# A two-layer encoder: one wide split in place of four, and the first pair of quads finished behind the second pair's second product

## The chip, the cores and the metric

The kernel runs on one core of a Trainium2 chip. The metric is device microseconds of one execution; lower is better. The core has five engines with queues of their own, each of which runs its instructions strictly in the order in which they were written for it: PE (matrix products), DVE and POOL (elementwise work), ACT (elementwise work with a table of functions, and copies out of PE's accumulators), and SP, which here only starts transfers. Between engines the order is kept by semaphores: an instruction whose operand isn't there holds everything behind it on its engine.

## The reference, cut to what matters

1024 tokens of width 1024 go through two layers. Each layer is a mixer (a Fourier group, windowed attention and attention to a memory, normed by groups and multiplied with `w_out`) and a gated feed-forward part, each between two RMS norms and with a residual:

```
for l in range(2):
    h = rmsnorm(x, g_pre_mix);  ...  x = x + rmsnorm(y @ w_out, g_post_mix)
    h = rmsnorm(x, g_pre_ffn[l])
    gate, up = split(h @ w_ffn_in[l])          # 1024 -> 2 * 2816
    x = x + rmsnorm((silu(gate) * up) @ w_ffn_out[l], g_post_ffn[l])
```

All is float32. The kernel multiplies float32 as three products of a faster type: each operand is split into `hi` (a cast on ACT) and `lo` (operand minus `hi`, on DVE), and PE adds hi·hi, hi·lo and lo·hi.

## The kernel before, in words

The feed-forward products go by a scheme of seven half-size products in place of eight (Strassen's). The normed activations, turned so that the 1024 features lie on partitions, are seven moving blocks `hb.b[1..7]` of 512 features by 512 tokens, each as hi and lo. Blocks 1, 2 and 3 are plain quarters, 5, 6, 7 and 4 are differences. Class `Blocks` (lines 1079 to 1123) makes them. `tile` turns one tile of 128 tokens; the first four tiles (half 0) are stored raw (`raw[0]`, `raw[1]`), the last four give blocks 5, 3 and 6 piece by piece. `plain` splits one 128-token piece of a raw quarter for block 1 or 2. `rest` makes blocks 7 and 4, four pieces each: a subtraction on DVE (line 1122), then cast and subtraction for hi and lo (lines 176 and 177).

A `Quad` (lines 1127 to 1217) is 256 columns of `w_ffn_in`. It does seven products in the order `ORDER = (1, 2, 5, 6, 3, 7, 4)`, each of 12 matmuls of 128x512. Ahead of a product `weights` makes its stationary operand: for 5, 6, 3 and 7 a running sum on DVE (line 1159), then again cast and `lo`, into a ring of slots `wcs` (four of them while the first two pairs run). A slot is only rewritten once the product that read it is done. `snap` copies an intermediate product out of the accumulator (ACT, line 1176) into a ring `sns`, and `step` combines them: lines 1208, 1211 and 1216 on DVE, 1205 and 1212 on POOL.

Two quads, gate and up, are a pair; there are 11 pairs a layer. `gate_out` (line 1223) takes silu of the gate quad's four results, `up_out` (lines 1227 to 1247) multiplies them with the up quad's, forms the seven blocks for the second product and sends them to memory `actd`.

The first two pairs overlap the end of the mixer. Per token tile the mixer's last product (`mo`, 24 matmuls) is followed by two norms: L1070, a square on ACT (L360), two small operations on POOL, L362, L363, a square on ACT (L314), POOL again, L319, and then PE turns the tile (`hTp`, line 1104). The products 1 and 2 of the first pair (`qc`) and of the second (`qa`) stand among the last tiles; then come 5 (`qy`), 6 (`qx`), 3 (into `qy`), 7 (into `qx`) and 4 (`qz`) of the first pair and of the second. The weights of the first pair are loaded by `load_part` (line 1136), where the destination has to come free first: a part of them into rows that the residual uses, the second pair's into the place of a weight of `mo`.

The order on each engine isn't the order of the source. A scheduler places each instruction by a model of the engines; `tc.issue_after(x)` keeps what is in it behind instruction x in the order. So an edit in one place can move instructions elsewhere, and what each queue holds is read from the built program, below.

## Time and profile before

| | |
|---|---|
| median of 3 runs | 2057.03 us (2054.72 to 2058.41) |
| profiled execution | 2054.33 us, of which the span of instructions is 2052.6 us |
| PE busy | 1994.2 us of the span (97%) |
| DVE, ACT, POOL busy | 1506.6, 1051.2, 699.9 us |
| mean granted clock of PE | 0.989 |
| layer 0: end of the mixer and first two pairs | about 385 to 480 us |
| layer 1: the same stage | about 1390 to 1480 us |

The profile is one execution. Times in it count from the first instruction. A row of the timeline has the start, the duration, the engine, the source line, the operation, and in brackets how long the engine sat idle before it and for what. A row of the stretches ("windows") has, for each engine, the busy time and the number of instructions, then the clock granted to PE (1.00 is full) and the DMA share.

### The profile page before, as it was taken

To read this page: it belongs to the slowest core of one execution; us is meant where nothing else is said; L and a number is where in the kernel's file an instruction comes from. 1 tells how busy PE (TensorE), PEld (TensorE's weight loads), DVE (VectorE), ACT (ScalarE), POOL (GpSimd) and SP (SyncE) were. 2 spreads that over 40 slices of the span, in tenths; PEclk is the share of its full clock that TensorE was granted. 3 is DMA by queue.
4 is the path that set the end of the run, shared out by engine and by line. 5 is a ranking of instruction groups with operands and counts; after the bars stand their busy time and mean duration, and the time that the engine had idled before them with its cause. 6 is when DMAs were issued, how large, how long until landed. Compare 5 with 4: busy or idle time off the path is not lost.

```text
span 2052.6 us, 28381 instructions
## 1 busy us (share of the span) xinstructions
PE 1994.2 (97%) x9587; PEld 1632.0 (80%) x9587; DVE 1506.6 (73%) x2400; ACT 1051.2 (51%) x2238; POOL 699.9 (34%) x819
## 2 busy tenths in 40 slices
PE   8999999999999999999999999999999999999998
PEld 7877777778888888887788768777788888887886
DVE  5557767897767766778866668578886777778766
ACT  6466767643333333554555667685333333345541
POOL 4354445234334333002423544451443433410011
PEclk9999999999999999999999999999999999999999
DMA  6110232433322323979831112243343233269973
GB/s 215 57 57 31 98 103 104 154 113 113 124 98 95 116 83 121 314 267 324 289 127 49 47 62 99 93 146 117 108 139 105 94 110 108 78 208 343 318 271 127
DMA packets 181890, 288.57 MB, mean 141 GB/s; under 512 B 15560, under 2 KB 81648, under 8 KB 181744
## 3 DMA queue, kind: packets, MB, share of 16 engines
q1 hardware_dynamic: 173680, 267.88, 39.0%
q10 hardware_dynamic: 8064, 18.88, 2.4%
q8 instruction: 75, 1.23, 0.2%
q14 instruction: 71, 0.58, 0.1%
HBM read 220.11 MB, written 66.58 MB: 140 GB/s over the span
## 4 chain that ended last, share of the span: by engine, by line
PE 81%; DVE 7%; DMA 4%; issue 3%; ACT 3%; POOL 2%; SPq 0%; DVEq 0%; POOLq 0%; ACTq 0%
PE fo L1319 15%; PE qy L1171 11%; PE qx L1171 11%; PE qc L1171 10%; PE mo L187 7%; PE qz L1171 6%; PE kvp L187 4%; PE qp L187 4%; PE zT L187 2%; DVE arena_r L177 2%; PE sc L785 2%; PE pT L822 2%; DMA arena_f<-actd 1%; PE av L830 1%; PE qa L1171 1%
## 5 line engine op out<-in xcount | busy, mean ns | idle before, releaser
L176 ACT CAST arena_r<-arena_f 128x512 fp32r<-128x512 f32 (+1 forms) x436 | 242.1, 582 | 323.7 <-DVE arena_f L1159 67.4
L1319 PE MATMUL fo<-arena_r 128*128 128x512 f32 x1512 | 353.8, 390 | 5.2 <-ACT big L1344 2.8
L177 DVE TENSOR_TENSOR arena_r<-arena_f,arena_r 128x512 fp32r<-128x512 f32 x354 | 254.5, 745 | 111.1 <-ACT arena_r L176 99.3
L1319 PEld LDWEIGHTS fo<-arena_r 128*128 128x128 f32 x1512 | 283.5, 188 | 64.9 <-ACT big L1344 3.2
L176 ACT CAST flex<-arena_f 128x512 fp32r<-128x512 f32 x210 | 128.7, 621 | 269.6 <-PE qy L1171 67.1
L1171 PE MATMUL qc<-arena_r,flex 128*128 128x512 f32 x912 | 221.0, 390 | 0.0
L1171 PEld LDWEIGHTS qc<-arena_r,flex 128*128 128x128 f32 x912 | 171.1, 188 | 36.8
L177 DVE TENSOR_TENSOR flex<-arena_f,flex 128x512 fp32r<-128x512 f32 x210 | 159.8, 767 | 51.9 <-ACT flex L176 51.1
L1205 POOL TENSOR_TENSOR arena_f<-arena_f 128x512 f32<-128x512 f32 x40 | 54.3, 1359 | 269.5 <-ACT arena_f L1176 269.5
L1171 PE MATMUL qy<-arena_r,flex 128*128 128x512 f32 x576 | 138.4, 390 | 0.0
L1171 PEld LDWEIGHTS qy<-arena_r,flex 128*128 128x128 f32 x576 | 108.0, 188 | 22.9 <-DVE flex L177 0.4
L1171 PE MATMUL qy<-arena_r 128*128 128x512 f32 x480 | 119.2, 397 | 5.4 <-DVE arena_r L177 5.4
L1171 PE MATMUL qx<-arena_r 128*128 128x512 f32 x360 | 119.3, 389 | 0.0
L1171 PEld LDWEIGHTS qy<-arena_r 128*128 128x128 f32 x480 | 91.7, 191 | 25.5 <-DVE arena_r L177 6.3
L1212 POOL TENSOR_TENSOR arena_f<-arena_f 128x512 f32<-128x512 f32 x40 | 66.8, 1670 | 129.6 <-DVE arena_f L1211 125.4
L1171 PE MATMUL qz<-arena_r,flex 128*128 128x512 f32 x320 | 107.4, 398 | 0.0
L1159 DVE TENSOR_TENSOR arena_f<-arena_f 128x512 f32<-128x512 f32 x90 | 97.5, 1084 | 8.5 <-DMA arena_f<-in_w_ffn_in 6.6
L177 POOL TENSOR_TENSOR arena_r<-arena_f,arena_r 128x256 fp32r<-128x256 f32 (+2 forms) x82 | 67.0, 823 | 99.9 <-ACT arena_r L176 74.5
L187 PE MATMUL mo<-big,arena_r 128*128 128x512 f32 x384 | 98.8, 398 | 1.4 <-DVE flex L859 1.3
L1171 PE MATMUL qx<-flex,flex 128*128 128x512 f32 x304 | 100.0, 390 | 0.0
L235 POOL TENSOR_SCALAR rrsv<-rss 128x1 f32<-128x1 f32 x32 | 10.7, 334 | 259.9 <-ACT arena_f L348 197.8
L1300 DVE TENSOR_TENSOR arena_f<-arena_f 128x512 f32<-128x512 f32 x110 | 80.1, 733 | 22.2 <-DMA arena_f<-in_w_ffn_out 21.1
(305 smaller groups left out, 4484.0 us busy)
## 6 DMA issues: line engine op xcount, KB each, us to landing
arena_f<-in_w_ffn_out SPq DMA_DIRECT2D x264, 256.0 KB, 4.6
actd<-arena_f SPq DMA_DIRECT2D x154, 256.0 KB, 2.5
arena_f<-actd SPq DMA_DIRECT2D x154, 256.0 KB, 4.3
arena_f<-in_w_ffn_in SPq DMA_DIRECT2D x46, 512.0 KB, 3.9
big<-in_w_ffn_in SPq DMA_DIRECT2D x40, 512.0 KB, 4.5
arena_f<-in_w_in SPq DMA_DIRECT2D x40, 256.0 KB, 2.9
arena_f<-in_x SPq DMA_DIRECT2D x16, 512.0 KB, 4.3
arena_f<-in_w_out SPq DMA_DIRECT2D x32, 256.0 KB, 2.7
```

What stands on the lines that cost most here:

```text
L176: nc.scalar.copy(hi, src)
L177: return (lo_eng or nc.vector).tensor_tensor(out=lo, in0=src, in1=f32(hi), op=ALU.subtract)
L187: mm(self.dst, a, b, start=self.i == 0, stop=self.i == self.n - 1)
L785: mm(pt, lhs, self.kst[g][i][:, k0 * P : k1 * P], start=i == 0, stop=i == 1)
L822: nc.tensor.transpose(pT[:, h, :], es_[h // 2][:, h % 2, j * P : j * P + P], ident)
L830: mm(av[64 * s : 64 * s + 64, 0 : 2 * P], self.v32[:, k0 + j], rhs, start=j == 0, stop=j == nk - 1)
L1159: nc.vector.tensor_tensor(out=s, in0=x, in1=y, op=op)
L1171: mm(pt, a, b, start=start and n == 0, stop=n == 11, skip_group_check=not start)
L1205: G(out=self.u2, in0=self.u2, in1=self.p1, op=ALU.add)
L1212: G(out=self.p5, in0=self.p1, in1=self.p5, op=ALU.add)
L1300: nc.vector.tensor_tensor(out=s, in0=x, in1=y, op=op)
L1319: mm(pt, ab[:, 0, x, sl], ab[:, 1, y], start=new and first and j == 0, stop=last and j == 2, skip_group_check=not new)
```

## The change

Four things are changed; what is computed stays the same.

1. `rest` makes a whole block with one subtraction of 128x2048 and one wide split, where four pieces of 128x512 had a subtraction and a split each. Block 2 is split whole in the same way (`whole`), behind the last of its tiles; block 1 still goes by pieces.
2. Silu and the products of the first pair are written between products 6 and 3 of the second pair's gate quad, and held behind the cast of the weights of product 6, where they stood behind the first pair. The copies' ring `sns` has eight places in place of six from the second pair on, so that the first pair's copies live on meanwhile.
3. For the first pair, the two additions of `step` that ran on POOL run on DVE.
4. The first running sum of the first pair (product 5) is held behind the last norm that has been written.

```diff
+    normed = [None]
     def norm_x(x, g, h=None, keep=None):
...
-        nc.vector.scalar_tensor_tensor(out=h, in0=x, scalar=r[:, 0:1], in1=g, op0=ALU.mult, op1=ALU.mult)
+        normed[0] = nc.vector.scalar_tensor_tensor(out=h, in0=x, scalar=r[:, 0:1], in1=g, op0=ALU.mult, op1=ALU.mult)
...
+        def whole(self, i, s):
+            self.b[i] = [big(4, 512) if k is None else at(k, 4, 512, dt=F32R) for k in self.HB[i]]
+            split(*self.b[i], s)
+
         def rest(self, kg):
-            for c in range(4):
-                d = self.raw[kg][:, :, c * P : c * P + P]
-                with tc.issue_after(self.lo.ins):
-                    nc.vector.tensor_tensor(out=d, in0=self.s[c], in1=d, op=ALU.subtract)
-                self.put((7, 4)[kg], c, d)
+            d = self.raw[kg]
+            cut = lambda ap: ap.rearrange("p k (c q) -> p k c q", q=P)
+            s = at(8, 4, 4, P).rearrange("p c k q -> p k c q")
+            with tc.issue_after(self.lo.ins):
+                nc.vector.tensor_tensor(out=cut(d), in0=s, in1=cut(d), op=ALU.subtract)
+            self.whole((7, 4)[kg], d)
...
-                nc.vector.tensor_tensor(out=s, in0=x, in1=y, op=op)
+                with tc.issue_after(normed[0].ins) if i == 5 and self.first else ExitStack():
+                    nc.vector.tensor_tensor(out=s, in0=x, in1=y, op=op)
...
-            split(w[:, 0], w[:, 1], s)
+            self.cast = nc.scalar.copy(w[:, 0], s)
+            nc.vector.tensor_tensor(out=w[:, 1], in0=s, in1=f32(w[:, 0]), op=ALU.subtract)
...
-            V, G = nc.vector.tensor_tensor, nc.gpsimd.tensor_tensor
+            V, G = nc.vector.tensor_tensor, (nc.vector if self.first else nc.gpsimd).tensor_tensor
...
             if p == 0:
-                gq, uq = first
-                g = gate_out(gq)
-                up_out(uq, g, actd, p)
-                wsums.ks, sns.ks = (4, 6, 0, 2), (36, 38, 40, 42, 32, 34)
+                wsums.ks, sns.ks, sns.i = (4, 6, 0, 2), (32, 34, 44, 46, 36, 38, 40, 42), 0
                 continue
...
                 for i in ORDER[2:] if p == 1 else ORDER:
+                    if i == 3 and p == 1 and q is gq:
+                        with tc.issue_after(q.cast.ins):
+                            g = gate_out(first[0])
+                        up_out(first[1], g, actd, 0)
                     q.step(i)
...
-                for c in range(4):
-                    hb.plain(1, c)
+                hb.whole(2, hb.raw[1])
```

Line numbers below are each program's own: the changed one's are higher, by 2 in the mixer (L364 is the old L362), by 8 to 11 in the quads (L1130 the wide subtraction, L1168 the running sum, L1171 and L1172 cast and lo of weights, L1181 the matmuls, L1215, L1218, L1221, L1222 and L1226 the old L1205, L1208, L1211, L1212 and L1216). In the rows, `flex_2276` holds the half-difference from which `rest` subtracts, `big_3523` and `big_3530` are the raw quarters, `big_4391` or `big_4376` is the lo of block 4, and `arena_r<-arena_f` or `flex_4102<-arena_f` at 128x512 is the lo of a weight.

The first place is DVE in layer 0 where `rest` runs. Before, from the weights of the first pair's product 4 to the weight of the second pair's product 5 (the last row):

```order
L177 TENSOR_TENSOR flex_4102<-arena_f,flex_4102 128x512
L177 TENSOR_TENSOR big_4391<-big_3530,arena_r 128x4x128
L1122 TENSOR_TENSOR big_3530<-flex_2276,big_3530 128x4x128
L1232 TENSOR_TENSOR arena_f<-qc_4147,flex_2276 128x512
L1208 TENSOR_TENSOR arena_f<-qy_4292,arena_f 128x512
L177 TENSOR_TENSOR flex_4102<-arena_f,flex_4102 128x512
L177 TENSOR_TENSOR big_4391<-big_3530,arena_r 128x4x128
L1122 TENSOR_TENSOR big_3530<-flex_2276,big_3530 128x4x128
L1159 TENSOR_TENSOR arena_f<-big_4579 128x512
L1211 TENSOR_TENSOR arena_f<-qx_4322,arena_f 128x512
L1159 TENSOR_TENSOR arena_f<-big_4579 128x512
L177 TENSOR_TENSOR arena_r<-arena_f,arena_r 128x512
```

The change, from the lo of a weight of product 3 on:

```order
L1172 TENSOR_TENSOR flex_4102<-arena_f,flex_4102 128x512
L177 TENSOR_TENSOR big_4032<-flex_2276,arena_r 128x4x128
L1130 TENSOR_TENSOR big_3523<-flex_2276,big_3523 128x2048
L1130 TENSOR_TENSOR big_3530<-flex_2276,big_3530 128x2048
L1168 TENSOR_TENSOR arena_f<-flex_3040,arena_f 128x512
L1172 TENSOR_TENSOR flex_4102<-arena_f,flex_4102 128x512
L177 TENSOR_TENSOR arena_r<-big_3523,flex_4303 128x2048
L1172 TENSOR_TENSOR flex_4102<-arena_f,flex_4102 128x512
L1168 TENSOR_TENSOR arena_f<-arena_f 128x512
L177 TENSOR_TENSOR big_4376<-big_3530,arena_r 128x2048
L1172 TENSOR_TENSOR arena_r<-arena_f,arena_r 128x512
L1215 TENSOR_TENSOR arena_f<-arena_f 128x512 x2
```

Blocks 7 and 4 are whole within eight instructions; before, their 16 pieces stood among the weights and sums of four products. The product of the first pair's up (L1232, now L1242) has left this stretch, the two L1215 have come into it.

The second place is PE in layer 1 at the mixer's last tile (`mo`). Before, from the turning of the tile that is two ahead of it:

```order
L1104 MATMUL hTp_12478<-const,arena_f 128x128 x4
L986 MATMUL ssp_12350<-const,arena_f 128x2 x2
L1171 MATMUL qc_12490<-arena_r,flex_12489 128x512 x2
L187 MATMUL mo_12426<-flex_4309,arena_r 128x512 x3
L187 MATMUL mo_12426<-arena_r 128x512 x6
L187 MATMUL mo_12426<-flex_4682,arena_r 128x512 x3
L1171 MATMUL qc_12490<-arena_r,flex_12489 128x512 x10
L187 MATMUL mo_12440<-flex_4309,arena_r 128x512 x3
L187 MATMUL mo_12440<-arena_r 128x512 x6
L187 MATMUL mo_12440<-flex_4682,arena_r 128x512 x3
L1171 MATMUL qc_12490<-arena_r 128x512 x2
L1171 MATMUL qa_12581<-arena_r,flex_12489 128x512 x2
```

The change:

```order
L187 MATMUL mo_12402<-flex_4303,arena_r 128x512 x3
L187 MATMUL mo_12402<-arena_r 128x512 x6
L187 MATMUL mo_12402<-flex_4658,arena_r 128x512 x3
L187 MATMUL mo_12416<-flex_4303,arena_r 128x512 x3
L187 MATMUL mo_12416<-arena_r 128x512 x6
L187 MATMUL mo_12416<-flex_4658,arena_r 128x512 x3
L1106 MATMUL hTp_12446<-const,arena_f 128x128 x4
L1106 MATMUL hTp_12454<-const,arena_f 128x128 x4
L1181 MATMUL qc_12466<-arena_r,flex_12465 128x512 x12
L1106 MATMUL hTp_12484<-const,arena_f 128x128 x4
L1181 MATMUL qa_12551<-arena_r,flex_12465 128x512 x2
L1181 MATMUL qc_12466<-arena_r 128x512 x12
```

The 24 matmuls of the last tile now run in one piece ahead of product 1 of the first pair, and the turning of the last tile but one (`hTp_12484`) stands ahead of the second pair's product 1 (`qa`). Layer 0 has the same move, with its `qc` in one piece behind `mo`.

The third place is DVE in layer 1 at the same time. Before:

```order
L177 TENSOR_TENSOR arena_r<-hTp_12478,arena_r 128x4x128
L1159 TENSOR_TENSOR arena_f<-arena_f 128x512 x2
L1070 SCALAR_TENSOR_TENSOR arena_f<-mo_12426,grs_12357,arena_f 128x512
L362 SCALAR_TENSOR_TENSOR arena_f<-arena_f,rrs_12391 128x1024
L177 TENSOR_TENSOR arena_r<-flex_10672,arena_r 128x4x128
L363 TENSOR_TENSOR arena_f<-arena_f 128x1024
L177 TENSOR_TENSOR arena_r<-arena_f,arena_r 128x512
```

The change, from the norm of the tile before on:

```order
L321 SCALAR_TENSOR_TENSOR arena_f<-arena_f,nrs_12283 128x1024
L177 TENSOR_TENSOR big_12395<-flex_10648,arena_r 128x4x128
L364 SCALAR_TENSOR_TENSOR arena_f<-arena_f,rrs_12367 128x1024
L365 TENSOR_TENSOR arena_f<-arena_f 128x1024
L1072 SCALAR_TENSOR_TENSOR arena_f<-mo_12402,grs_12333,arena_f 128x512
L1172 TENSOR_TENSOR arena_r<-arena_f,arena_r 128x512
L1172 TENSOR_TENSOR arena_r<-flex_11412,arena_r 128x512
```

The two running sums of product 5, which need weights from memory, stood ahead of the last two tiles' norms; they now stand behind the last norm, some twenty instructions on.

More of the change, by code (lines that the diff above doesn't have):

```diff
@@ L1116, in tile, with __init__ @@
                     self.put(6, c, self.s[c])
+        def whole(self, i, s):
+            self.b[i] = [big(4, 512) if k is None else at(k, 4, 512, dt=F32R) for k in self.HB[i]]
+            split(*self.b[i], s)
         def rest(self, kg):
-            for c in range(4):
-                d = self.raw[kg][:, :, c * P : c * P + P]
-                with tc.issue_after(self.lo.ins):
-                    nc.vector.tensor_tensor(out=d, in0=self.s[c], in1=d, op=ALU.subtract)
-                self.put((7, 4)[kg], c, d)
+            d = self.raw[kg]
[4 more added lines that the diff above has]
+            self.whole((7, 4)[kg], d)
     ORDER = (1, 2, 5, 6, 3, 7, 4)
     class Quad:
-        def __init__(self, l, c0, hb):
-            self.hb, self.c0, self.a = hb, c0, {}
+        def __init__(self, l, c0, hb, first=False):
+            self.hb, self.c0, self.a, self.first = hb, c0, {}, first
             self.w = T["w_ffn_in"][l]
@@ L1249, in quads @@
     def quads(l, p, hb):
-        return [Quad(l, j * DFF + 2 * p * P, hb) for j in range(2)]
+        return [Quad(l, j * DFF + 2 * p * P, hb, p == 0) for j in range(2)]
     def ffn_in(l, hb, actd, first, second):
```

## The prediction

> **What bounds the kernel now.** I read the page first, then the stretches of 5 us to find where PE stands, then PE's timeline there, and last DVE, POOL, ACT and SP in the same microseconds. The page says that PE is the bound nearly everywhere:
>
> ```profile
> PE 1994.2 (97%) x9587; PEld 1632.0 (80%) x9587; DVE 1506.6 (73%) x2400; ACT 1051.2 (51%) x2238; POOL 699.9 (34%) x819
> ```
>
> No matmul is added or removed, so all that can change is the 58 us of the span in which PE stands, and the time at half clock that follows. At the places that the change touches, the stretches show both (columns: busy time and count of PE, PEld, DVE, ACT, POOL, then PE's clock and the DMA share):
>
> ```profile
> 430.00:435.00 5.00, 4.54 (x21) 3.42 (x19) 5.00 (x10) 2.35 (x5) 2.84 (x1) 1.00 0.14 52
> 435.00:440.00 5.00, 2.19 (x5) 1.80 (x6) 5.00 (x7) 1.00 (x2) 2.57 (x3) 0.66 0.00 0
> 440.00:445.00 5.00, 5.00 (x16) 3.90 (x16) 4.10 (x4) 1.28 (x3) 4.53 (x3) 0.66 0.58 162
> ...
> 1395.00:1400.00 5.00, 1.83 (x7) 0.84 (x5) 4.13 (x5) 0.62 (x1) 0.00 (x0) 0.92 0.74 205
> 1400.00:1405.00 5.00, 3.59 (x9) 2.82 (x10) 5.00 (x8) 2.92 (x5) 1.80 (x3) 0.50 0.26 105
> ...
> 1445.00:1450.00 5.00, 2.86 (x13) 2.02 (x13) 5.00 (x7) 0.62 (x1) 5.00 (x2) 1.00 0.03 13
> 1450.00:1455.00 5.00, 4.14 (x13) 2.70 (x12) 5.00 (x6) 2.18 (x4) 3.09 (x3) 0.66 0.28 86
> ```
>
> In three places PE is short of work while DVE is busy in all 5.00 of 5 us or just before it, and the clock falls to half behind each. PE's timeline gives the waits:
>
> ```profile
> 388.79 0.73 PE L1171 MATMUL qa<-arena_r,flex 128*128 128x512 f32 x2 [1.24 <-ACT flex L176]
> 391.22 2.56 PE L1171 MATMUL qc<-arena_r 128*128 128x512 f32 x10 [1.21 <-DVE arena_r L177]
> 393.62 2.43 PE L1171 MATMUL qa<-arena_r,flex 128*128 128x512 f32 x10
> 412.16 5.60 PE L1171 MATMUL qy<-arena_r,flex 128*128 128x512 f32 x24
> 437.81 4.63 PE L1171 MATMUL qy<-arena_r 128*128 128x512 f32 x10 [3.27 <-DVE arena_r L177]
> 448.06 0.39 PE L1171 MATMUL qz<-arena_r,flex 128*128 128x512 f32 x1
> ...
> 1394.75 0.84 PE L187 MATMUL mo<-flex,arena_r 128*128 128x512 f32 x3
> 1398.62 0.78 PE L1171 MATMUL qa<-arena_r,flex 128*128 128x512 f32 x2 [2.58 <-ACT flex L176]
> 1401.41 4.63 PE L1171 MATMUL qc<-arena_r 128*128 128x512 f32 x10 [2.01 <-DVE arena_r L177]
> 1448.95 3.47 PE L1171 MATMUL qy<-arena_r 128*128 128x512 f32 x10 [2.14 <-DVE arena_r L177]
> 1454.14 0.50 PE L1171 MATMUL qz<-big,flex 128*128 128x512 f32 x1 [0.86 <-DVE big L177]
> 1459.02 0.39 PE L1171 MATMUL qz<-arena_r,flex 128*128 128x512 f32 x1
> ```
>
> A matmul starts every 0.227 us at full clock (24 take 5.60 less the 0.17 of the last one's drain). Ten take 2.43, but 4.63 behind the 3.27 and behind the 2.58 and 2.01, and 3.47 behind the 2.14: the half clock costs 2.2, 2.2 and 1.0 more. So layer 0 loses 1.24 + 1.21 + 3.27 + 2.2 = 7.9 us here, layer 1 2.58 + 2.01 + 2.2 + 2.14 + 1.0 + 0.86 = 10.8. These 18.7 us are nearly all that the change can win.
>
> **The change part by part.** Why DVE is late in layer 0:
>
> ```profile
> 399.20 1.22 DVE L363 TENSOR_TENSOR arena_f<-arena_f 128x1024 f32<-128x1024 f32 x1
> 415.07 0.69 DVE L1122 TENSOR_TENSOR big<-flex,big 128x512 f32<-128x512 f32 x1
> 415.67 0.69 DVE L177 TENSOR_TENSOR flex<-arena_f,flex 128x512 fp32r<-128x512 f32 x1
> 436.01 1.74 DVE L177 TENSOR_TENSOR arena_r<-arena_f,arena_r 128x512 fp32r<-128x512 f32 x1
> 440.08 1.77 DVE L177 TENSOR_TENSOR big<-big,arena_r 128x512 fp32r<-128x512 f32 x1
> 435.50 1.71 POOL L1212 TENSOR_TENSOR arena_f<-arena_f 128x512 f32<-128x512 f32 x1
> 439.64 1.65 POOL L1212 TENSOR_TENSOR arena_f<-arena_f 128x512 f32<-128x512 f32 x1 [2.43 <-ACT arena_r L176]
> ```
>
> The pieces of `rest` run from 415.07 to 441.85, and the weight split for which PE waits, at 436.01, is queued behind them. An instruction of 128x512 takes 0.69 and the next starts 0.60 later, but 1.74 and 1.77 where one of POOL runs: it ends about half a microsecond after POOL's, so one overlap costs DVE 1.06.
>
> *Fewer, wider instructions.* The wide form isn't in this trace. From 512 to 1024 elements the time goes from 0.69 to 1.22, so 2048 take at least 0.69 + 3 x 0.53 = 2.28 (the next starts after 2.2), and at most four of the small, 2.76. The first is the nearer, since both its rows are of the same operation. Four small starts are 2.4; five such merges a layer (two subtractions, three splits) save 5 x 0.2 = 1.0 us of DVE, at worst lose 5 x 0.36 = 1.8. On ACT the cast goes the same way. [...]
>
> *Additions from POOL to DVE.* Four a layer; each costs DVE 0.60 and spares an overlap of 1.06: 4 x 0.46 = 1.8 us of DVE.
>
> *Order in layer 0.* The wide subtractions can't start before the split ahead of them, whose cast waits for the gate's 12 of `qy`; PE interleaves the two `qy`, so that is after 13 matmuls: 412.16 + 13 x 0.227 = 415.1, cast and two splits more, 417.2 for the first subtraction. From there DVE runs two wide (4.4), two small, one wide (lo of block 7 at 425.0), two small, one wide: lo of block 4 at 428.4, where 441.85 stands now. PE, from 412.16, has 24 of `qy`, 24 of `qx` and 24 of product 3: 72 x 0.227 = 16.3, to 428.5. So the first matmuls of 7 and 4 find their blocks. 48 more of these bring PE to 439.4. The weight of the second pair's product 5 is split behind L1221, which waits for `qx` to end (434.8): 436.3, ahead of PE by 3 us. With its 12 matmuls PE is at 442.1; now the same 132 matmuls end at 448.3 (448.06 and its 0.23). The gain is 6.2 us: the wait, its half clock, and the row's few tenths.
>
> *Ahead of it in layer 0.* With `qc` in one piece behind `mo`, the 1.24 stays (the cast of the next weight waits for the slot that `qc` reads), while the split behind the 1.21 comes earlier. I take 1.0.
>
> *Order in layer 1.*
>
> ```profile
> 1384.83 0.85 PE L187 MATMUL mo<-flex,arena_r 128*128 128x512 f32 x3
> 1388.50 1.06 ACT L360 ACTIVATE arena_f<-arena_f 128x1024 bf16<-128x1024 f32 x1 [0.81 <-DVE arena_f L1070]
> 1390.97 0.55 POOL L237 TENSOR_TENSOR rrs<-rrsv,const 128x1 f32<-128x1 f32 x1
> 1392.71 0.84 PE L187 MATMUL mo<-flex,arena_r 128*128 128x512 f32 x3
> 1393.58 0.99 SPq L1136 DMA_DIRECT2D flex<-in_w_ffn_in  x2
> 1397.95 0.62 ACT L176 CAST flex<-flex 128x512 fp32r<-128x512 f32 x1 [4.45 <-DMA flex<-in_w_ffn_in]
> 1394.27 0.69 DVE L1159 TENSOR_TENSOR arena_f<-arena_f 128x512 f32<-128x512 f32 x1 [3.34 <-DMA arena_f<-in_w_ffn_in]
> 1397.14 1.28 DVE L362 SCALAR_TENSOR_TENSOR arena_f<-arena_f,rrs 128x1024 f32<-128x1024 f32 x1
> 1400.18 1.06 ACT L314 ACTIVATE arena_f<-arena_f 128x1024 f32<-128x1024 f32 x1 [1.62 <-DVE arena_f L363]
> ```
>
> Two late loads make the waits of 2.58 and 2.01. The second pair's weights go to a place that `mo` reads until 1393.4; they are issued at 1393.58 and cast at 1397.95. And the running sum L1159 waits 3.34 for its weights, at the head of DVE's queue; L362 and the norm of a tile, and the split for `qc`, wait behind it. In the change the sums stand behind the last norm, and `mo` runs in one piece: its 24 matmuls from about 1386.2 (the tile before ends at 1385.5, four small ones follow) end at 1391.6, the place is free at 1389.6, and the load, 4.4 us from issue to cast here, is there at 1394. The next wait is the turning of the last tile but one, behind a chain: its first square is at 1388.5 and POOL is done at 1391.5, as now; then L364 and L365 to 1393.8, two L1072 and two splits meanwhile to 1396.1, the second square and POOL as long, the norm to 1397.4. PE is there at 1391.6 + 1.0 (eight turnings) + 2.7 (12 of `qc`) = 1395.3 and waits about 2.2 us. The split for the second pair's product 1 comes six DVE instructions and a tile's L364 and L365 later, at about 1403.1, and PE is there at 1401.7: 1.4. From there PE has no wait that I can find, and ends the first 24 of `qy` at 1425.9, the same 132 matmuls further on at 1450.4, where now 1459.25 stands: 8.9. The 2.2 us wait lies near the 2.14 that halved the clock, so I take off 1.0 for that: 7.9. [...]
>
> *Deferred silu and products.* Nothing is added; two L1242 and the two sums stand behind the weights of the second pair's product 6, from 440 us on, and five instructions of POOL with them. If all five block DVE, 5 x 1.06 = 5.3 us. They do that now too, ten microseconds earlier, where DVE is full. From 466 us DVE has idle time:
>
> ```profile
> 468.48 0.69 DVE L177 TENSOR_TENSOR flex<-big,flex 128x512 fp32r<-128x512 f32 x1 [1.93 <-ACT flex L176]
> 470.89 0.69 DVE L1208 TENSOR_TENSOR arena_f<-qy,arena_f 128x512 f32<-128x512 f32 x1 [1.71 <-PE qy L1171]
> ```
>
> So I cost it at nothing; if that cover is gone, PE waits up to 5.3 a layer. The ring of eight copies costs nothing: PE isn't late for a copy in any of the waits.
>
> *Sum.* Layer 0: 6.2 + 1.0 = 7.2; layer 1: 7.9; together 15.1. Working along the queues finds only the waits that I looked for; each layer has one of 1.2 here that I couldn't have named (the 1.24 and 1.21), so I take off 1.5 a layer: 12. The profiled execution had 2054.33 (its span 2052.6 and 1.7 around it), so 2042.3 by its own time; it lies 2.7 under the median of the runs. The four executions together have a mean of 2056.1, and 2056.1 - 12 gives **2044**.
>
> **The rivals.**
>
> *Displaced stalls.* In layer 1 the wait for a load becomes a wait for the norm chain, with the half clock behind it (2.2 + 1.4 + 2.2, near the 2.58 + 2.01 + 2.2 = 6.8 of now). For it: L364 stands behind ACT's square and POOL either way. Then layer 1 gains only 2.14 + 1.0 + 0.86 = 4.0, and 7.2 + 4.0 - 3 = 8.2: 2048.
>
> *The wide pieces come late.* Four pieces let DVE, ACT and DVE work in turn; a wide block is there only after all three, and the first now stands behind a split that waits for `qy`. If lo of block 4 comes 4 us later than 428.4, PE waits at the first matmuls of 7 and 4, the half clock behind it costs 2.2, and the 6.2 us in layer 0 are gone; the same in layer 1 takes its later 4.0 and about 1 more. 12 - 6.2 - 5 leaves 1: 2055. Against it: between 428.4 and PE's third matmul of product 4 is only half a microsecond, but each delay is paid once.
>
> *Slower.* The deferred products fall on the stretch where DVE prepares the second pair's products 3, 7 and 4. It decides if less than 5.3 us of DVE time is spare from 440 to 455: then PE waits 5.3 and half clock follows, 2.2: 7.5 a layer, 15 in all, against the 12: 2059. Against it: DVE has saved 2.8 us by then and reaches the stretch earlier.
>
> **How the numbers follow.** The forecast has 0.58 and a range of its own of 2038 to 2050 (18 of the 18.7 won at the one end, half of the 12 at the other). Displaced stalls 0.22, late pieces 0.12, slower 0.08. The range reaches from 2036, all of the 18.7 and 1.4 more if the wide forms save what the merges could at most, to 2056, no gain. A measurement here can tell about 0.2%, 4 us, from no change. Forecast and displaced stalls are both faster by more than that: 0.80. Late pieces: within it, 0.12. Slower: 0.08.
>
> **What would show it.** In layer 0, PE without a wait over 1 us between the first `qy` and the last `qz`, at full clock; DVE's wide rows at 2.28, POOL idle in that stretch; in layer 1, no wait for a load at the head of DVE and a wait of about 2 us at `hTp`. It is wrong if PE waits for lo of block 7 or 4, if a wait of over 2 us stands in the second pair's gate quad, or if the clock is still at half for more than 10 us between 1390 and 1460.

## The result, and the profile after

| | before | changed |
|---|---|---|
| median of six runs | 2057.03 us (2053.14 to 2058.41) | 2045.81 us (2040.79 to 2047.99) |
| ratio | | 0.9944, 95% interval 0.993 to 0.9959 |
| profiled execution, and its span | 2054.33 us, 2052.6 us | 2045.68 us, 2043.9 us |

The changed kernel is 11.2 us faster; 2044.0 was forecast. A second measurement gave 0.9948 (0.9929 to 0.9968). The page has the busy times of the changed kernel:

```profile
PE 1990.0 (97%) x9587; PEld 1630.4 (80%) x9587; DVE 1499.5 (73%) x2378; ACT 1047.9 (51%) x2220; POOL 691.9 (34%) x811
```

PE's busy time falls by 4.2 us though its 9587 matmuls are the same: less of it is run at half clock (the granted clock is below 1.00 in 40 of the span's stretches of 1 us, in 51 of them before). PE's timeline of the changed kernel, at the places that the prediction went through:

```profile
405.98 6.05 PE L1181 MATMUL qy<-arena_r,flex 128*128 128x512 f32 x24
423.88 0.39 PE L1181 MATMUL qz<-big,flex 128*128 128x512 f32 x1
433.62 2.88 PE L1181 MATMUL qy<-arena_r 128*128 128x512 f32 x12
436.34 0.39 PE L1181 MATMUL qx<-arena_r 128*128 128x512 f32 x1
...
452.06 0.74 PE L1181 MATMUL qx<-arena_r,flex 128*128 128x512 f32 x2 [1.50 <-DVE flex L1172]
...
1395.82 0.66 PE L1106 MATMUL hTp<-const,arena_f 128*128 128x128 f32 x4 [2.27 <-DVE arena_f L321]
1397.59 1.22 PE L1181 MATMUL qa<-arena_r,flex 128*128 128x512 f32 x2 [1.11 <-ACT flex L1171]
1398.61 3.88 PE L1181 MATMUL qc<-arena_r 128*128 128x512 f32 x12
1447.33 2.43 PE L1181 MATMUL qy<-arena_r 128*128 128x512 f32 x10
1465.48 0.74 PE L1181 MATMUL qx<-arena_r,flex 128*128 128x512 f32 x2 [1.02 <-DVE flex L1172]
```

In layer 0 the 132 matmuls from the first `qy` to the second pair's twelfth run from 405.98 to 436.34 without a wait: 30.4 us, where they took 36.1 before. In layer 1 the two late loads have become one wait of 2.27 at the turning, 1.11 behind it, and a half clock (0.50 from 1398 to 1400) that makes 12 matmuls last 3.88 where others take 2.88. Where no clock is given below, a half clock is read from such lengths. Both layers have a new wait at product 6 of the second pair's up quad. (The rows tell the product: block 6 is read as `arena_r` and `big`, block 7 as `flex` and `arena_r`. The expectations below call it product 7.)

Where is the gain? A whole layer can be cut at two places that are easy to find in every kernel of this study: its first score matmul (`sc`) and the first matmul of its second feed-forward product (`fo`). PE's timeline of the kernel before, and then of the changed one:

```profile
208.31 0.98 PE L785 MATMUL sc<-arena_r 128*128 128x256 f32 x6
817.60 2.66 PE L1319 MATMUL fo<-arena_r 128*128 128x512 f32 x11
1215.37 0.48 PE L785 MATMUL sc<-arena_r 128*128 128x256 f32 x2
1829.57 10.82 PE L1319 MATMUL fo<-arena_r 128*128 128x512 f32 x47
```

```profile
204.15 0.98 PE L787 MATMUL sc<-arena_r 128*128 128x256 f32 x6
807.40 11.04 PE L1330 MATMUL fo<-arena_r 128*128 128x512 f32 x48
1213.31 0.49 PE L787 MATMUL sc<-arena_r 128*128 128x256 f32 x2
1820.88 19.43 PE L1330 MATMUL fo<-arena_r 128*128 128x512 f32 x85
```

From `sc` to `fo` layer 0 takes 603.3 us in place of 609.3, layer 1 607.6 in place of 614.2. So 6.0 + 6.6 = 12.7 us are won in the two layers, and 4.0 are lost outside of them, where the change does nothing (833.1 us against 829.1). These two lengths, a single execution each, are compared below. Two executions of the changed kernel differ in them by 1.1 and 1.5 us, so smaller differences can't be told.

### The profile page after: what moved, and what is told of

It reads as the page before. It is cut to its first block, busy times and chain, and to the rows that moved or that the text cites. A ratio compares the mean times of both kernels' runs of the same rounds, so it can differ in the third digit from the quotient of the medians.

```text
span 2043.9 us, 28334 instructions
## 1 busy us (share of the span) xinstructions
PE 1990.0 (97%) x9587; PEld 1630.4 (80%) x9587; DVE 1499.5 (73%) x2378; ACT 1047.9 (51%) x2220; POOL 691.9 (34%) x811
## 3 DMA queue, kind: packets, MB, share of 16 engines
q8 instruction: 75, 1.23, 0.2%
## 4 chain that ended last, share of the span: by engine, by line
PE 84%; DVE 5%; DMA 3%; ACT 3%; POOL 2%; issue 2%; SPq 0%; DVEq 0%; POOLq 0%; ACTq 0%
PE fo L1330 17%; PE qy L1181 11%; PE qx L1181 11%; PE qc L1181 11%; PE mo L187 7%; PE qz L1181 6%; PE qp L187 4%; PE kvp L187 4%; PE zT L187 2%; PE sc L787 2%; PE pT L824 2%; PE qa L1181 1%; PE mav L932 1%; PE av L832 1%; PE av L839 1%
## 5 line engine op out<-in xcount | busy, mean ns | idle before, releaser
L176 ACT CAST arena_r<-arena_f 128x512 fp32r<-128x512 f32 (+2 forms) x344 | 185.5, 571 | 181.9 <-DMA arena_f<-actd 76.1
L1181 PE MATMUL qc<-arena_r,flex 128*128 128x512 f32 x912 | 220.5, 390 | 0.0
L1171 ACT CAST flex<-arena_f 128x512 fp32r<-128x512 f32 x148 | 91.9, 621 | 225.6 <-PE qy L1181 66.4
L1181 PEld LDWEIGHTS qc<-arena_r,flex 128*128 128x128 f32 x912 | 171.0, 188 | 36.8
L1181 PE MATMUL qy<-arena_r,flex 128*128 128x512 f32 x576 | 139.9, 390 | 0.0
L1171 ACT CAST arena_r<-arena_f 128x512 fp32r<-128x512 f32 x92 | 57.1, 621 | 160.7 <-DVE arena_f L1168 71.1
L1172 DVE TENSOR_TENSOR flex<-arena_f,flex 128x512 fp32r<-128x512 f32 x148 | 112.7, 762 | 27.4 <-ACT flex L1171 27.3
L1215 POOL TENSOR_TENSOR arena_f<-arena_f 128x512 f32<-128x512 f32 x36 | 48.3, 1342 | 231.8 <-ACT arena_f L1186 231.8
L1181 PEld LDWEIGHTS qy<-arena_r,flex 128*128 128x128 f32 x576 | 107.8, 188 | 23.1 <-DVE arena_r L177 0.4
L1181 PE MATMUL qx<-arena_r 128*128 128x512 f32 x360 | 119.3, 389 | 0.0
L1181 PE MATMUL qy<-arena_r 128*128 128x512 f32 x480 | 116.1, 389 | 0.0
L1172 DVE TENSOR_TENSOR arena_r<-arena_f,arena_r 128x512 fp32r<-128x512 f32 x92 | 68.2, 741 | 61.5 <-ACT arena_r L1171 61.2
L1181 PE MATMUL qz<-arena_r,flex 128*128 128x512 f32 x320 | 106.5, 395 | 0.0
L1181 PEld LDWEIGHTS qy<-arena_r 128*128 128x128 f32 x480 | 90.1, 188 | 18.7
L1168 DVE TENSOR_TENSOR arena_f<-arena_f 128x512 f32<-128x512 f32 x90 | 97.3, 1085 | 7.3 <-DMA arena_f<-in_w_ffn_in 5.6
L1222 POOL TENSOR_TENSOR arena_f<-arena_f 128x512 f32<-128x512 f32 x36 | 60.0, 1667 | 124.5 <-DVE arena_f L1221 124.5
L235 POOL TENSOR_SCALAR rrsv<-rss 128x1 f32<-128x1 f32 x32 | 14.8, 463 | 257.3 <-ACT arena_f L350 195.8
L1242 POOL TENSOR_TENSOR arena_f<-arena_f,flex 128x512 f32<-128x512 f32 x32 | 54.4, 1701 | 137.8 <-DVE arena_f L1218 53.8
```

The costliest lines, as they stand in the source:

```text
L176: nc.scalar.copy(hi, src)
L1168: nc.vector.tensor_tensor(out=s, in0=x, in1=y, op=op)
L1171: self.cast = nc.scalar.copy(w[:, 0], s)
L1172: nc.vector.tensor_tensor(out=w[:, 1], in0=s, in1=f32(w[:, 0]), op=ALU.subtract)
L1181: mm(pt, a, b, start=start and n == 0, stop=n == 11, skip_group_check=not start)
L1215: G(out=self.u2, in0=self.u2, in1=self.p1, op=ALU.add)
```

## The experiments

Two sets show what the parts are worth: the changed kernel with one part undone, and the kernel before with one part alone. A third set comes from what the first showed. Each ratio is to the kernel before, measured beside it: its median was 2055.46 us beside e1 to e4, 2052.71 beside e5 to e8 and 2056.57 beside e9 to e12, so medians of different sets aren't compared. The lengths are one profile's.

| kernel | median, us | ratio (95%) | layer 0, us | layer 1, us |
|---|---|---|---|---|
| before | | 1 | 609.3 | 614.2 |
| changed | 2045.81 | 0.9944 (0.993 to 0.9959) | 603.3 | 607.6 |
| changed, again (e5) | 2043.68 | 0.9948 (0.9929 to 0.9968) | 604.3 | 609.1 |
| undone: wide forms (e1) | 2044.83 | 0.995 (0.9938 to 0.9962) | 605.1 | 606.1 |
| undone: deferral (e2) | 2046.1 | 0.9959 (0.9946 to 0.9971) | 605.5 | 606.7 |
| undone: held sum (e3) | 2049.42 | 0.997 (0.9959 to 0.9981) | 603.8 | 611.4 |
| undone: sums on DVE (e4) | 2048.1 | 0.9965 (0.995 to 0.998) | 606.5 | 610.8 |
| alone: wide forms (e9) | 2051.01 | 0.9973 (0.9963 to 0.9983) | 607.1 | 611.7 |
| alone: held sum (e10) | 2047.68 | 0.9961 (0.9946 to 0.9976) | 607.4 | 606.3 |
| alone: sums on DVE (e11) | 2053.81 | 0.999 (0.998 to 1.0) | 610.7 | 612.0 |
| alone: deferral (e12) | 2049.52 | 0.9971 (0.9959 to 0.9984) | 608.0 | 612.5 |
| changed, block 2 in pieces (e6) | 2039.3 | 0.9932 (0.9914 to 0.9951) | 604.8 | 606.0 |
| changed, deferred products on DVE (e7) | 2039.54 | 0.9925 (0.9905 to 0.9944) | 602.2 | 605.3 |
| both of these (e8) | 2037.3 | 0.9917 (0.9893 to 0.994) | 604.1 | 601.7 |

By the clock, e3, e9, e11 and e12 came out within the range of their theory, e10 and e5 just under theirs, and e6, e7 and e8 under theirs by 1.7, 2.5 and 0.7 us. In e1 the time lies under both ranges, in e2 and e4 between the two.

### One part undone

**e1**, `rest` and block 2 in four pieces again:

```diff
-            s = at(8, 4, 4, P).rearrange("p c k q -> p k c q")
-            with tc.issue_after(self.lo.ins):
-                nc.vector.tensor_tensor(out=cut(d), in0=s, in1=cut(d), op=ALU.subtract)
-            self.whole((7, 4)[kg], d)
+            for c in range(4):
+                ...
+                self.put((7, 4)[kg], c, d)
...
-                hb.whole(2, hb.raw[1])
+                for c in range(4):
+                    hb.plain(1, c)
```

> The changed kernel, but blocks 7, 4 and 2 are again made in four pieces each. Theory of the prediction (DVE's time sets the first pair, and the wide form brings blocks 7 and 4 early): the lo of block 4 is again the 39th DVE instruction behind the last piece of block 6, at about 435 us in layer 0, ten microseconds later than now, so PE waits 2 to 4 us in the first pair's products 7 and 4 or at the second pair's first product, with half clock behind it; 3 to 6 us a layer, 2050 to 2056. Rival, only the 1.0 us of DVE's time that the merges save counts: DVE has a spare of that size, 2046 to 2048. A third point: the changed kernel is 3.5 us ahead already at 200 us, where none of the four edits stands, and the order on PE, DVE and ACT differs between 190 and 330 us. With pieces that order is the old one word for word. If the order is the cause, 3.5 us come back here in the first 200 us, and 2049 is the least that is to be seen; if it was the one execution, nothing comes back there.

The lo of block 4 is late as expected (DVE and PE of e1):

```profile
432.69 0.69 DVE L177 TENSOR_TENSOR big<-big,arena_r 128x512 fp32r<-128x512 f32 x1
433.35 0.50 PE L1180 MATMUL qx<-arena_r 128*128 128x512 f32 x1 [1.07 <-ACT arena_r L1170]
433.93 0.39 PE L1180 MATMUL qz<-big,flex 128*128 128x512 f32 x1
```

It ends at 433.4 where the changed kernel has 422.5 (420.22 and its 2.28, below). But PE doesn't wait for it: the first matmul that reads it (`qz<-big`, 433.93) finds it, since in the order built the second pair's first product (at 428.89) stands ahead, and the 1.07 us just before are for the cast of a weight. The theory was too dear by a factor of two or three in layer 0 (it loses 1 to 2 us), and layer 1 is even 1.5 to 3 us shorter than with the wide forms: there the wait of 2.27 us at the turning is gone. Neither of the two stories had that, and e6 follows it up. The time, 0.995, can't be told from the changed kernel's 0.9944 and 0.9948.

The third point also fell. The first score matmul is at 204.15 in the changed kernel, and in e5, the same program, and e1, with the old order up to there:

```profile
209.12 0.98 PE L787 MATMUL sc<-arena_r 128*128 128x256 f32 x6
```

```profile
204.38 0.98 PE L787 MATMUL sc<-arena_r 128*128 128x256 f32 x6
```

The early 4 us belong to the single execution, not to the order.

**e2**, silu and products where they were, ring of six:

```diff
             if p == 0:
+                gq, uq = first
+                g = gate_out(gq)
+                up_out(uq, g, actd, p)
-                wsums.ks, sns.ks, sns.i = (4, 6, 0, 2), (32, 34, 44, 46, 36, 38, 40, 42), 0
+                wsums.ks, sns.ks = (4, 6, 0, 2), (36, 38, 40, 42, 32, 34)
...
-                    if i == 3 and p == 1 and q is gq:
-                        with tc.issue_after(q.cast.ins):
-                            g = gate_out(first[0])
-                        up_out(first[1], g, actd, 0)
```

> The changed kernel, but silu and products of the first pair stand behind the first pair again, with a ring of six copies. Theory (the five POOL instructions lengthen DVE's by 1.06 us each where DVE is full): PE waits 2 to 4 us at the second pair's first product in each layer, with half clock behind one of them; the waits of 1.50 us in layer 0 and 1.02 us in layer 1 at the second pair's product 7, which the changed kernel has, are gone; 2049 to 2054. Rival (DVE has saved enough by the other edits, and the deferral itself makes the two new waits): no wait above 1 us at the second pair's first product, 2042 to 2045.

```profile
458.39 0.50 PE L1181 MATMUL qx<-arena_r,flex 128*128 128x512 f32 x1 [2.89 <-ACT flex L1171]
```

No wait at the second pair's first product, as the rival had it. But the wait at product 6 of the up quad, which the rival put down to the deferral, is there without it, and larger (2.89 in layer 0; layer 1 has 1.09 at product 4). It has another cause: the cast for which PE waits stands on ACT behind a silu of the second pair, which waits 7.09 us for an addition on POOL (L1222). So a wait at this place needs no deferral; what the deferral costs is read from e7.

**e3**, the first sum not held:

```diff
-                with tc.issue_after(normed[0].ins) if i == 5 and self.first else ExitStack():
+                with ExitStack():
```

> The changed kernel, but the first running sum isn't held behind the last norm. Its order has the sum ahead of two norms again in layer 1, though the last tile's 24 matmuls stay in one piece. Theory (a load at the head of DVE's queue holds the norms): DVE waits 1.5 to 3.5 us for the load of the sum's weights near 1393 us, PE's wait for the turning of the last tile but one grows from 2.27 us to 4 to 5 us; 2 to 4 us more, 2048 to 2051. Rival (the chain of norms is as late anyway, and the load has landed): no wait for a load, PE's wait within 0.5 us of 2.27, 2045 to 2047.

DVE and PE of e3, layer 1:

```profile
1391.32 0.69 DVE L1168 TENSOR_TENSOR arena_f<-arena_f 128x512 f32<-128x512 f32 x1 [1.35 <-DMA arena_f<-in_w_ffn_in]
1395.76 1.22 PE L1181 MATMUL qa<-arena_r,flex 128*128 128x512 f32 x2 [4.69 <-ACT flex L1171]
1397.49 4.59 PE L1181 MATMUL qc<-arena_r 128*128 128x512 f32 x12
```

The load at the head of DVE's queue is back (1.35 us, just under the theory's range), PE waits 4.69, and the half clock costs 1.7 (4.59 against 2.88). The place is not the turning but the second pair's product 1 (`qa`): the cast of its weights stands on ACT behind a tile's square, which waits 2.42 us for DVE. Layer 1 loses 2 to 4 us, layer 0 nothing, so the theory holds in its cause and its price.

**e4**, the first pair's additions on POOL:

```diff
-            V, G = nc.vector.tensor_tensor, (nc.vector if self.first else nc.gpsimd).tensor_tensor
+            V, G = nc.vector.tensor_tensor, nc.gpsimd.tensor_tensor
```

> The changed kernel, but the additions of the first pair's step run on POOL again. Theory (1.8 us of DVE's time a layer, and DVE is ahead of PE by several us at that place): eight DVE rows of about 1.7 us beside POOL's come back, but PE has no new wait above 1 us; 2045 to 2047. Rival (what PE waited for was the overlap with POOL): a wait of 1 to 3 us with half clock at the second pair's first product in both layers; 2049 to 2055.

```profile
446.88 0.73 PE L1181 MATMUL qz<-arena_r 128*128 128x512 f32 x2 [2.48 <-DVE arena_r L1172]
```

The new wait is larger than the theory allowed, but later than the rival put it: not at the second pair's first product, but at its product 4, where DVE has rows of 1.75 to 1.77 us one behind the other. Both layers are 2 to 3 us longer than in the changed kernel. DVE wasn't so far ahead that 1.8 us more didn't matter.

### What the changed kernel still loses

e1 had no wait at the turning in layer 1. ACT and DVE of the changed kernel, where block 2 is split whole there:

```profile
1374.05 1.89 ACT L176 CAST arena_r<-big 128x2048 fp32r<-128x2048 f32 x1
1376.11 1.07 ACT L362 ACTIVATE arena_f<-arena_f 128x1024 bf16<-128x1024 f32 x1
1375.98 2.29 DVE L177 TENSOR_TENSOR arena_r<-big,arena_r 128x2048 fp32r<-128x2048 f32 x1 [1.24 <-ACT arena_r L176]
1378.98 1.74 DVE L364 SCALAR_TENSOR_TENSOR arena_f<-arena_f,rrs 128x1024 f32<-128x1024 f32 x1
...
1394.48 1.28 DVE L321 SCALAR_TENSOR_TENSOR arena_f<-arena_f,nrs 128x1024 f32<-128x1024 f32 x1
```

The wide cast stands ahead of a tile's square (L362) on ACT, and the wide split ahead of L364 on DVE: the norm chain of this tile goes through both. And DVE, ACT's neighbour in the chain, waits 1.24 for the wide cast itself. The turning for which PE waits is that of the tile behind it, whose last norm is the row at 1394.48. The other suspect is POOL. DVE and then POOL of the changed kernel in layer 0:

```profile
411.20 4.49 DVE L1130 TENSOR_TENSOR big<-flex,big 128x2048 f32<-128x2048 f32 x2
...
420.22 2.28 DVE L177 TENSOR_TENSOR big<-big,arena_r 128x2048 fp32r<-128x2048 f32 x1
...
441.30 1.77 DVE L1172 TENSOR_TENSOR flex<-arena_f,flex 128x512 fp32r<-128x512 f32 x1
...
444.69 1.77 DVE L1172 TENSOR_TENSOR arena_r<-arena_f,arena_r 128x512 fp32r<-128x512 f32 x1
...
451.32 0.68 DVE L1172 TENSOR_TENSOR flex<-arena_f,flex 128x512 fp32r<-128x512 f32 x1
```

```profile
433.61 5.34 POOL L1242 TENSOR_TENSOR arena_f<-arena_f,flex 128x512 f32<-128x512 f32 x2 [38.08 <-DVE arena_f L1222]
439.03 3.49 POOL L1252 TENSOR_TENSOR arena_f<-arena_f 128x512 f32<-128x512 f32 x2
442.60 1.62 POOL L1256 TENSOR_TENSOR arena_f<-arena_f 128x512 f32<-128x512 f32 x1
```

From 439.6 to 446.4 DVE runs four instructions of 1.77 beside POOL's, and from there to the split at 451.32, for which PE waits at 452.06, it has next to no idle time.

**e5** is the changed kernel as it is, run beside the three that follow.

> The changed kernel as it is, beside the next three on one chip: 2044 to 2048, since it had 2045.8 in six runs. Its profile is a second execution: if the 3.5 us that it was ahead at 200 us and the 7 us that it lost between 1020 and 1170 us belong to the one execution, they are different here; if they belong to the program, they are there again. The wait of about 2.3 us at the turning of the last tile but one in layer 1, and the waits of 1.5 and 1.0 us at the second pair's product 7, should be there again, since they come from the order on DVE.

The waits at the turning (2.29) and behind it (1.11) and at layer 1's product 6 (1.02) are there again, layer 0's has 1.07 in place of 1.50. Behind the same two waits at the head of layer 1 the half clock lasts longer, by the length of the 12 matmuls, 5.28 us in place of 3.88:

```profile
1398.69 5.28 PE L1181 MATMUL qc<-arena_r 128*128 128x512 f32 x12
```

Most of what was lost outside of the layers isn't lost here: 830.4 us in place of 833.1, against 829.1 before. So it belongs to the execution.

**e6**, block 2 alone in pieces:

```diff
-                hb.whole(2, hb.raw[1])
+                for c in range(4):
+                    hb.plain(1, c)
```

> The changed kernel, with block 2 alone split in four pieces again (blocks 7 and 4 stay wide). Theory: in layer 1 the wide split of block 2 (2.29 us on DVE, behind a wide cast) stands ahead of a tile's norm and delays the chain to the turning of the last tile but one; in pieces it doesn't, PE's wait of 2.27 us there falls under 0.7 us, and the wait of 1.11 us and the half clock behind it go: 3 to 4 us in layer 1, nothing in layer 0: 2041 to 2044. Rival (what the kernel with all pieces won in layer 1 came from blocks 7 and 4 in pieces): the wait of 2.27 us stays, 2045 to 2047.

**e7**, the first pair's deferred products on DVE:

```diff
-        V, G = nc.vector, nc.vector if p == NFF // 2 - 1 else nc.gpsimd
+        V, G = nc.vector, nc.vector if p in (0, NFF // 2 - 1) else nc.gpsimd
```

> The changed kernel, with the five POOL instructions of the first pair's deferred products on DVE. Theory (POOL beside DVE makes an instruction of DVE 1.77 us in place of 0.69): DVE gets 5 x 0.60 = 3.0 us and loses up to 5 x 1.06 = 5.3 us a layer; no row of 1.7 us between 438 and 446 us, and the waits of 1.50 us (layer 0) and 1.02 us (layer 1) at the second pair's product 7 go: 2042 to 2045. Rival (the instructions that are added delay the weights as much as the overlap did): waits of 1 us or more at the second pair's products 7 or 4 stay in both layers, 2045 to 2048.

**e8**, both edits.

> Block 2 in pieces and the deferred products on DVE together. If both theories hold, the gains stand in different places and add up: 2038 to 2042. If only block 2 counts, 2041 to 2044; if neither, 2045 to 2048.

In e6 the wait at the turning is gone and layer 1 is 1.6 to 3.1 us shorter, as the theory said, though a wait of 1.78 at `qa` and one of 2.20 late in the stage take a part of the 3 to 4 us back. The theory's mechanism is another matter, below. In e7 neither layer has a wait at the second pair's product 6 or 4 any more, and all six times (up to 2039.73) lie under all six of e5 (from 2040.65). DVE's rows there are short (0.69 where the changed kernel has 1.77), and the one wait left in layer 1 is that for a weight's cast (DVE in layer 0, PE in layer 1):

```profile
444.22 0.69 DVE L1172 TENSOR_TENSOR arena_r<-arena_f,arena_r 128x512 fp32r<-128x512 f32 x1
1395.90 1.06 PE L1181 MATMUL qa<-arena_r,flex 128*128 128x512 f32 x2 [3.15 <-ACT flex L1171]
```

Layer 0 is 1.1 to 2.2 us shorter than in the changed kernel, layer 1 2.2 to 3.8. In e8 they add up in layer 1, which is 5.9 to 7.4 us shorter; in layer 0 (604.1) they don't, with waits of 0.90 and 0.54 us back in the second pair's product 6. DVE and PE of e8:

```profile
1375.74 1.29 DVE L364 SCALAR_TENSOR_TENSOR arena_f<-arena_f,rrs 128x1024 f32<-128x1024 f32 x1 [0.72 <-POOL rrs L237]
1395.34 1.28 DVE L321 SCALAR_TENSOR_TENSOR arena_f<-arena_f,nrs 128x1024 f32<-128x1024 f32 x1
1394.21 2.56 PE L1181 MATMUL qc<-arena_r 128*128 128x512 f32 x10 [0.55 <-DVE arena_r L1172]
1397.07 1.04 PE L1106 MATMUL hTp<-const,arena_f 128*128 128x128 f32 x8
```

The same tile's L364 runs at 1375.74 in place of 1378.98, and the turning has no wait. But the first does not explain the second. The first score of layer 1 is at 1213.14 here and at 1213.31 in the changed kernel, so the two timelines can be laid side by side; and the next tile's last norm, for which the turning waits, starts at 1395.34, 0.9 us later than the 1394.48 above. e6 has it at 1394.56, with its first score 1.0 us earlier. What differs is the order on PE. With block 2 in pieces 12 more matmuls of `qc` and two of `qa` stand ahead of the turning, and PE gets there only at 1397.07. The kernels tell the two orders apart: those with the held sum and pieces (e1, e6, e8, e10) wait 0.54 or 0.55 us at `qc` and not at the turning, and all with block 2 whole wait 2.27 us or more at the turning or at `qa`.

With 2037.3 us e8 is the fastest kernel of the study, 6.4 us under the changed one's median beside it (2043.68); by their ratios to the kernel before the two intervals still touch.

### One part alone

**e9**, wide forms alone (the first diff above, the other way round, on the kernel before).

> The kernel before with the wide forms alone (blocks 7, 4 and 2). Theory (parts stand in for one another: each of three makes DVE early enough in layer 0, and only the held sum helps at the head of layer 1): the wait of 3.27 us and its half clock in layer 0 go, 4 to 6 us; in layer 1 the sum's load still holds the norms and block 2's wide split makes it no better, so a wait of 4 to 5 us stays there: 2049 to 2053. Rival (additive, the merges are worth 1.0 us of DVE's time a layer): the wait of 3.27 us falls to 2 to 2.5 us only, 2054 to 2056.

```profile
444.93 4.15 PE L1181 MATMUL qy<-arena_r,flex 128*128 128x512 f32 x10 [2.19 <-DVE flex L1172]
...
1400.26 0.85 PE L1181 MATMUL qa<-arena_r,flex 128*128 128x512 f32 x2 [3.91 <-ACT flex L1171]
```

In layer 0 the rival's wait stands there, 2.19 and a half clock (4.15 against 2.43), a little later; the 3.27 has shrunk and moved on, not gone. Layer 1 is nearly as the theory had it, 3.91 where 4 to 5 us were to stay.

**e10**, the held sum alone (that of e3).

> The kernel before with the first running sum held behind the last norm, alone. Theory: in layer 1 the waits of 2.58 and 2.01 us at the first pair's and second pair's product 1 and the half clock of 2.2 us behind them go (under 1 us each is left); the 2.14 us at block 4's stretch may stay; in layer 0 the wait of 3.27 us stays: 2048 to 2052. Rival (the norm chain takes the load's place, as the prediction had it for the whole change): a wait of 2 us or more stays at the turning or at product 1, 2053 to 2056.

```profile
435.61 2.57 PE L1180 MATMUL qy<-arena_r 128*128 128x512 f32 x10 [1.71 <-DVE arena_r L1171]
440.78 0.50 PE L1180 MATMUL qz<-big,flex 128*128 128x512 f32 x1 [1.49 <-DVE big L177]
...
1396.44 2.56 PE L1180 MATMUL qc<-arena_r 128*128 128x512 f32 x10 [0.54 <-DVE arena_r L1171]
...
1468.75 0.50 PE L1180 MATMUL qz<-arena_r 128*128 128x512 f32 x1 [2.65 <-ACT arena_r L1170]
```

The theory holds in layer 1: 2.58, 2.01 and their half clock are gone (the mean clock from 1380 to 1500 is 1.00), 0.54 is left, and nothing waits at the turning. Layer 1 is 7.9 us shorter by this edit alone: more than by the whole change (5.1 to 6.6), by about what two executions differ in or somewhat more. In layer 0 the 3.27 was to stay; it is 1.71 and 1.49 in its place, without a half clock (1.00 from 380 to 480).

**e11**, the additions on DVE alone (that of e4).

> The kernel before with the first pair's additions on DVE, alone. Theory: 1.8 us of DVE's time a layer, so the wait of 3.27 us in layer 0 falls to 1 to 2 us and its half clock goes at best; the 2.14 us of layer 1 falls under 1 us; the waits at the head of layer 1 stay: 2050 to 2054. Rival (the additions on DVE delay the weights by as much as the overlap did): both waits within 0.5 us of the old, 2055 to 2057.

```profile
387.55 4.02 PE L1180 MATMUL qc<-arena_r 128*128 128x512 f32 x10 [1.17 <-DVE arena_r L1171]
...
435.96 0.73 PE L1180 MATMUL qz<-arena_r,flex 128*128 128x512 f32 x2 [1.10 <-ACT arena_r L176]
```

The waits came out as the theory had them (1.10 in layer 0; 0.59 where layer 1 had 2.14), but 2053.81 is 0.1% less than before, not told from nothing. In the profile a half clock at 387.55 (4.02 for ten matmuls; 0.66 from 388 to 392), which the kernel before didn't have behind the same two waits, eats what layer 0 won.

**e12**, the deferral alone (that of e2).

> The kernel before with silu and products of the first pair deferred, and the ring of eight, alone. Theory: the five POOL instructions leave the full stretch, so the wait of 3.27 us goes in layer 0 and the 2.14 us in layer 1, and a wait of 1 to 2 us comes at the second pair's products 7 or 4 in each layer; the waits at the head of layer 1 stay: 2049 to 2053. Rival (they cost as much later as they did earlier): two waits of 2 us or more in place of the old, 2055 to 2058.

```profile
433.70 2.56 PE L1180 MATMUL qy<-arena_r 128*128 128x512 f32 x10 [1.14 <-DVE arena_r L1171]
438.29 0.50 PE L1180 MATMUL qz<-big,flex 128*128 128x512 f32 x1 [1.57 <-DVE big L177]
```

The theory roughly: 3.27 falls to 1.14, 2.14 to 1.07, and a new wait of 1.57 comes in both layers, but it is for block 4, not for a weight; the loads' waits stay.

## Why the prediction was right, point by point

**The two layers.** Layer 0's first pair was to gain 6.2 us between the first `qy` and the second pair's twelfth; the timeline has 36.13 - 30.36 = 5.8. DVE's wide pieces came as costed (2.28 each), and PE reached the lo of block 4 at 423.88, 1.4 us behind its end at 422.5, with no wait: the rival of late pieces fell. All of it stands some 6 us earlier than by the prediction's clock: 4.2 us since this execution reached its first scores earlier, the rest won ahead of the first `qy`, where 1.0 was forecast. In layer 1 the wait at the turning is 2.27 (2.2 forecast), and the half clock costs 1.0 (1.0); that the second agrees is luck, since in e5 it costs 2.4 behind the same waits. Counted from the layer's first score, the second pair's twelfth `qy` ends 7.6 us earlier than before (7.9 forecast). Per layer 7.2 - 1.5 = 5.7 and 7.9 - 1.5 = 6.4 were forecast; the two profiles have 6.0 and 5.0, 6.6 and 5.1.

**Displaced stalls**, the rival with 0.22, is in part what layer 1 shows: a wait for the norm chain in place of the loads. It is 2.27 + 1.11 + 1.0 in place of 6.8, not nearly the same.

**The step that failed** is "Deferred silu and products. Nothing is added ... So I cost it at nothing". The cover it named begins at 466; the products run from 434 on, and DVE is busy nearly without a gap until 457.9. The price is 1.5 us in layer 0 and 1.0 us in layer 1 as waits, and by e7 1.1 to 2.2 and 2.2 to 3.8 us of the layers' length; none of this passes the bound of 5.3 that the prediction kept. The 1.5 us a layer "for waits not seen" is about what it took, so the sum came out right with a wrong term in it, and that the two are of a size is luck. The "slower" rival had the place and the mechanism right (four rows of DVE that take 4.3 us more), but not its price, 7.5 us a layer.

**A term with the wrong sign**: "five such merges a layer ... save 1.0 us of DVE" counts block 2 among them. In layer 1 e6 is 1.6 to 3.1 us shorter without that merge. The 2.2 us wait that the prediction read out of the order came with this edit, and through the order: the merge delays one tile's norm by 3.2 us (1378.98 against 1375.74), but not the norm for which PE waits. Nor is the 1.0 us of DVE's time to be seen: e1, with 30 instructions more, has DVE busy for 1497.5 us, the two executions of the changed kernel for 1499.5 and 1500.8 (rows beside POOL's, 1.77 in place of 0.69, move this figure too). And no run shows the 1.4 us more for the merges with which the range reaches down to 2036: in the changed kernel two wide rows of layer 0 take 4.41 us up to the start of the next row (411.20 to 415.61) where eight starts of 0.60 take 4.8, so 0.2 a merge, as costed.

**Which part does it.** The prediction gave each part a price but the stages one gain. In layer 1 the held sum alone wins more than the whole change, and the other three together give some of it back. In layer 0 no part alone wins over 2.2 us, and undoing one loses some 3 us at most: each takes a little of DVE's time out of the full stretch, and PE's wait moves on to the next weight or block that is late. That is why 3.27 never vanishes by one part; it goes to 2.19, to 1.71 and 1.49, to 1.14 and 1.57, to 1.10 and smaller ones.

What stays open: why the scheduler builds the one order with block 2 whole and the other with block 2 in pieces. In the kernels with pieces PE also has 10 matmuls of `qc` between the last two halves of `mo`, which the changed kernel runs in one piece. No run kept the wide split and took that order, so it isn't shown that the order alone would win the 1.6 to 3.1 us.

## What to carry to other kernels

Merging small instructions into a wide one can cost more than it saves, and on another engine than the one that was looked at: here that of block 2 (1.6 to 3.1 us of layer 1 by e6) came with an order on PE in which a turning that wasn't ready stood ahead of a product that could be run first. So compare the built order of every queue, and check that a delay which the merge causes is one that the bottleneck waits for. Work on one engine that makes a neighbour's instructions longer (here POOL's, beside which four of DVE's took 1.77 us in place of 0.69) is not hidden because its own result isn't needed; ask whether the neighbour has idle time in exactly those microseconds. And look for an instruction that waits for a load at the head of a queue: here, on DVE (1.35 us in e3, with 4.69 of PE's behind it), holding it back won 7.9 us of a layer alone, and leaving that out of the whole change lost 2 to 4.

## What the hardware showed that wasn't expected

In these runs the wait's length doesn't tell whether the clock falls to half behind it. Behind 1.24 and 1.21 us before (391.22) ten matmuls took 2.56 (the clock is 1.00 from 391 to 394), behind 1.23 and 1.17 in e11 they took 4.02 (0.66 from 388 to 392), with the same matmuls at the same place. Behind e10's 2.65 at 1468.75 the clock stayed at 1.00 (1468 to 1480); behind the 2.27 and 1.11 of the changed kernel it fell (0.50 from 1398 to 1400), for 12 matmuls of 3.88 us in one execution and of 5.28 in the other. So here the price of a half clock is a chance, not a sum. What sets it off is not shown.

What lies outside of the two lengths took 826.9 to 833.1 us in the fourteen profiles: 204.2 to 209.5 ahead of the first scores, 397.1 to 405.9 from layer 0's second product to layer 1's scores, 219.6 to 225.1 at the end; two executions of the same program (the changed kernel) are 6.1 us apart in the second of these. So one execution's span tells a change of 10 us poorly, unless it is cut at such marks first.
